# The first attention's probabilities times values: three key blocks of 128, or two of 128 and one of 64-key rests with high and low parts stacked

## The chip, the cores and the metric

The kernel runs on one core of a Trainium2 chip. A core has a matrix engine (TensorE, "PE" in the profile, with its weight loads as "PEld"), a vector engine (VectorE, DVE), a scalar engine (ScalarE, ACT), GpSimd (POOL) and a sync engine (SyncE, SP), which here issues most transfers. The engines run side by side, each through its own queue in order, and wait for one another through semaphores. The metric is the device time of one launch in microseconds; lower is better.

## The reference

One layer of an encoder on 2048 tokens of width 1024: a norm, a projection to queries, keys, values and gates, two attentions, a gated merge, and a feed-forward part. The change lies in the first attention, `windowed_gqa`: 8 query heads of 64 elements share 2 key/value heads, and each query sees the keys at most 128 tokens away.

```python
def block(i):                                   # 128 queries
    qi = qb[:, i]
    ki = lax.dynamic_slice_in_dim(kp, i * A_BLOCK, 3 * A_BLOCK, axis=1)
    vi = lax.dynamic_slice_in_dim(vp, i * A_BLOCK, 3 * A_BLOCK, axis=1)
    dist = jnp.abs(q_pos[:, None] - k_pos[None, :])
    valid = (dist <= A_WINDOW) & (k_pos[None, :] >= 0) & (k_pos[None, :] < s)
    sc = jnp.einsum('bqkgd,bskd->bkgqs', qi, ki) * scale - slopes * dist
    sc = jnp.where(valid, sc, -jnp.inf)
    p = softmax(concatenate([sc, sink_col], -1))[..., :-1]
    return jnp.einsum('bkgqs,bskd->bqkgd', p, vi)
```

A block of 128 queries thus meets 384 keys: the block before it, its own, and the one after it.

## The kernel before, in words

Float32 accuracy is made from pieces: an operand is split into a high part (a copy by ScalarE to a rounded type) and a low part (the rest, a subtraction by VectorE), and the products of the parts are added up in PSUM, the matrix engine's accumulator banks.

The stages follow one another: the input projection for the first half of the tokens (0 to about 360 us), the first attention (to about 646 us), the second attention, and the merge and the feed-forward part. The projection of the second half of the tokens is cut into 68 tiles (24 matmuls of 512 columns each, lines 203 to 205) that serve as filler: `paced` (line 838) hands them out among the attention's blocks, each behind the last product of an earlier block or unit, through the list `done`. In the second attention the first five tiles have no such condition, and the sixth waits for the first unit's last product. The instructions are traced in program order, and an automatic scheduler with a model of times then writes each engine's queue; the order of a queue is thus not the order of the code.

The first attention has 32 units, one for each of two key/value heads `g` and 16 query blocks `i`. `attn_a(g, i)` (line 763) has two phases, and `drive` (line 828) starts the second phase of a unit after the first phase of the unit two later.

- Phase one: the queries are loaded (line 773), reordered by GpSimd (line 774), and put into four groups `u` of 32 queries, each with the four heads of its `g`, so that a group fills 128 rows. Group `u` sees the 288 keys from 32u to 32u + 288 of the 384. Its scores are two matmuls (line 784); VectorE adds the bias and finds the maximum (line 786), ScalarE takes the exponential (line 791), and GpSimd multiplies by the reciprocal of the sum (line 795). The tile `s` has 4 x 384 columns, and what a group doesn't see stays zero.
- Phase two: for each of the three key blocks `c` (two for the first and the last query block), four transposes, one for each `u`, bring 128 keys into the rows and 4 x 128 queries into the columns (line 802). ScalarE copies the high part `ph` (line 805), VectorE makes the low part `pl` (line 806), and two products of 512 columns with the values of that block follow, one for each part (lines 807 and 808). The values' tile holds 64 columns of high and 64 of low parts, so the two halves of the result's rows are added at the end (lines 813 and 814).

Buffers lie in two stacks that grow towards each other in each of SBUF's 128 partitions, one from the left, one from the right. In the first attention the left one holds, above the projection's pages: `ka1`, `va1`, `qraw`, `qa`, `sta`, `sa`, `ya`, `ph`, `pl`, `biasa1`, `byhead`; the right one, next to the filler's weight pools: `biasa0`, `va0`, `ka0`. The second attention's right stack starts at the same weight pools: `masks` (12.5 KB per partition), `kb0` (16), `qb0` (2), `braw0` (2), `biass0` (4), `stb` (0.5), `biass1` (4), `qb1` (2), `qb2` (2), `biasl` (5), `braw1` (2), `kb1` (16). A tile that lies where an earlier one lay waits until that one is no longer read. `biass0` and `biass1` are the short bias tables that GpSimd fills (line 915) for the first and the second unit of the second attention, `qb0` and `qb1` their queries (line 934); its scores are line 947, its scalings line 963, its transposes line 975 and its products line 987.

Of the kernel before, what the change touches and what calls it, by code (L numbers as in the profile page):

```python
# [8 lines left out]
F32 = mybir.dt.float32  # L9
F32R = mybir.dt.float32r  # L10
AF = mybir.ActivationFunctionType
ALU = mybir.AluOpType
# [10 lines left out]
P = 128  # L23
# [72 lines left out]
def encoder_layer(ctx, tc, x, norm_mix, w_in, b_gate, sink, rpb, w_pa, w_pb, w_out,  # L96
                  norm_mlp, w_up, w_down, norm_final, dist_a, mask_b, out):
    nc = tc.nc
    V, A, G, PE, SY = nc.vector, nc.scalar, nc.gpsimd, nc.tensor, nc.sync
# [9 lines left out]
    def pools(stack, side, tags, name):  # L109

        return {t: pool(f"{name}_{t}", side=side, stack=stack) for t in tags}
# [9 lines left out]
    def psum(tag, bufs):  # L121
        n_ps[0] += 1
        return pps[tag].tile([P, 512], F32, tag=tag, bufs=bufs, name=f"{tag}_{n_ps[0]}")
# [3 lines left out]
    def T(pl, shape, dt, tag, bufs):  # L127
        n_t[0] += 1
        pl = pl[tag] if isinstance(pl, dict) else pl
        return pl.tile(shape, dt, tag=tag, bufs=bufs, name=f"{tag}_{n_t[0]}")  # L130


    ident = cp.tile([P, P], F32, name="ident")
# [441 lines left out]
    for p in range(2):  # L575
        t = T(xp, [P, D], F32, "xin", 8).rearrange("p (k c) -> p k c", k=4)
        c = QUADS[2][0]
# [93 lines left out]
    s_h = ExitStack()  # L671
    hpl = [pool(f"hT{n}", side="left", stack=s_h) for n in range(4)]
    s_a = ExitStack()
    ap_ = pools(s_a, "left", ("ka1", "va1", "qraw", "qa", "sta", "sa", "ya", "ph", "pl", "biasa1", "byhead"), "a")
    ap_.update(pools(s_a, "right", ("biasa0", "va0", "ka0"), "a"))
    hp = {}

# [53 lines left out]
    for h in range(4):  # L731
        at = slice(h * A_Q, (h + 1) * A_Q)
# [22 lines left out]
    def load_kv(g, m, behind=None):  # L755
        k, kd = kas[g][:, :, m * (S // 2) : (m + 1) * (S // 2)], ks_a[m][g]
        with tc.issue_after(behind) if behind else nullcontext():
# [2 lines left out]
            SY.dma_start(k[64:128, 1].bitcast(F32), kd[0:64])  # L760
            SY.dma_start(vas[g][:, 8 * m : 8 * m + 8].bitcast(F32), vs_a[m][g])

    def attn_a(g, i):
        c0, c1 = (1 if i == 0 else 0), (2 if i == 15 else 3)
        if bias_a[g] is None:

            with tc.issue_after(shares[2]):
                make_bias_a(g)
        base = (i - 1) * P
        by_head = T(ap_, [P, 4, P], F32, "qraw", 3)  # L770
        q = T(ap_, [P, 4, 4, A_Q], F32R, "qa", 2)
        s = sas[len(began) % 4]
        began.append(SY.dma_start(by_head, qs_a[g][i // 8][:, :, i % 8]).ins)
        G.tensor_copy(out=q.rearrange("p u h q -> p h u q"), in_=by_head.rearrange("p h (u q) -> p h u q", u=4))
        ka, v = kas[g], vas[g]
        st = T(ap_, [P, 8, 4], F32, "sta", 8)
        mx, nm, sm, es, ri = (st[:, k, :] for k in range(5))
        sink_g = sink_p[:, g : g + 1]
        span = [(max(u * A_Q, c0 * P), min(u * A_Q + A_K, c1 * P)) for u in range(4)]
        for u, (lo, hi) in enumerate(span):  # L780
            n = hi - lo
            ps = psum("s", 3)
            for z in range(2):
                PE.matmul(ps[:, :n], q[:, u].rearrange("p h q -> p (h q)"), ka[:, z, base + lo : base + hi],
                          start=z == 0, stop=z == 1)
            V.tensor_tensor_reduce(out=s[:, u, lo:hi], in0=ps[:, :n], in1=bias_a[g][:, lo - u * A_Q : hi - u * A_Q],
                                   scale=1.0, scalar=sink_g, op0=ALU.add, op1=ALU.max, accum_out=mx[:, u : u + 1])
        A.activation(nm, mx, AF.Copy, scale=-1.0)
        A.activation(es, mx, AF.Exp, bias=sink_g, scale=-1.0)
        for u, (lo, hi) in enumerate(span):  # L790
            A.activation(s[:, u, lo:hi], s[:, u, lo:hi], AF.Exp, bias=nm[:, u : u + 1], accum_out=sm[:, u : u + 1])
        V.tensor_tensor(out=sm, in0=sm, in1=es, op=ALU.add)
        V.reciprocal(ri, sm)
        for u, (lo, hi) in enumerate(span):
            share = G.tensor_scalar(s[:, u, lo:hi], s[:, u, lo:hi], ri[:, u : u + 1], 1.0, ALU.mult, ALU.mult)
        shares.append(share.ins)
        yield
        po = psum("av", 1)
        for c in range(c0, c1):
            pt = psum("pt", 2)  # L800
            for u in range(4):
                PE.transpose(pt[:, u * P : (u + 1) * P], s[:, u, c * P : (c + 1) * P], ident)  # L802
            ph = T(ap_, [P, 512], F32R, "ph", 3)
            pl = T(ap_, [P, 512], F32R, "pl", 3)
            A.copy(ph, pt)
            V.tensor_tensor(out=pl, in0=pt, in1=ph.bitcast(F32), op=ALU.subtract)
            PE.matmul(po, v[:, i - 1 + c, :], ph, start=c == c0, stop=False)
            last = PE.matmul(po, v[:, i - 1 + c, :], pl, start=False, stop=c == c1 - 1).ins
        done.append(last)
        t = T(ap_, [64, 512], F32, "ya", 2)  # L810
        t4 = t.rearrange("d (h u q) -> d h u q", h=4, u=4)
        by_u = po.rearrange("p (u h q) -> p h u q", u=4, h=4)
        A.copy(t4, by_u[64:128])
        V.tensor_tensor(out=t4, in0=by_u[0:64], in1=t4, op=ALU.add)
        flush(queue=SY)
        put(y_a[g].rearrange("(h d) t -> d h t", d=64)[:, :, i * P : (i + 1) * P],
            t.rearrange("d (h q) -> d h q", h=4))
# [838 lines left out]
```

## Time and profile before

| | |
|---|---|
| median of 3 runs | 2607.2 us (2606.03 to 2607.28) |
| profiled execution | 2605.6 us, span 2603.8 us |
| granted clock of TensorE | 0.999 |
| busy share of the span | PE 99%, DVE 62%, ACT 47%, POOL 14% |
| first attention, transposes (line 802) | 368 |
| first attention, products (lines 807 and 808) | 92 and 92 |

The span runs from the first to the last instruction of one profiled execution; the device time is a little longer. "Busy" of TensorE counts overlapping matmuls as one stretch, so the distance between the starts of two matmuls tells more than their durations. A group's row gives line, engine, operation, the tiles written and read, the shape and the count, and then either the least, median and greatest duration in ns with the first and last start in us, or the busy time in us with the mean in ns and the idle time before it. A timeline row gives the start, the duration from the first start to the last end of so many like instructions in a row, and, in brackets, the idle time before them and who ended it.

### The profile page before, as it was taken

The page shows a single profiled execution, that of the slowest core. Times are in us where ns is not written, and L with a number is a line of the kernel's source. Part 1 is how long each engine was busy: PE and PEld are TensorE (multiplying, and loading weights), DVE is VectorE, ACT ScalarE, POOL GpSimd, SP SyncE. Part 2 cuts the span into 40 slices and gives each one's busy share as a digit, 9 for nine tenths or more (in the row PEclk, how much of TensorE's full clock was granted, in tenths as well). Part 3 has the DMA queues.
Part 4 walks back from the last instruction along what each step waited for, and adds up shares of the span by engine and source line. Part 5 has one row for each costly group of instructions (what it writes and reads, how often), then busy time and mean ns, then how long its engine had stood idle before and what let it go on. Part 6 is the DMA issues. An engine that isn't in the chain of part 4 may idle for free.

```text
span 2603.8 us, 34627 instructions
## 1 busy us (share of the span) xinstructions
PE 2571.4 (99%) x12140; PEld 2143.3 (82%) x12140; DVE 1608.0 (62%) x2621; ACT 1232.4 (47%) x2261; POOL 368.1 (14%) x493
## 2 busy tenths in 40 slices
PE   8999999999999999999999999999999999999999
PEld 6888788788888888888888888888888888888887
DVE  8865666665544444665478677766656535554766
ACT  5334356666555555542335544644444322323454
POOL 1000124444655541000000000100000000000010
PEclk9999999999999999999999999999999999999999
DMA  5657486465975745865466665854428825445555
GB/s 185 203 155 202 132 260 166 119 167 154 247 212 173 207 140 188 273 202 161 143 198 207 238 222 200 306 173 146 158 100 313 290 97 186 146 148 167 186 193 171
DMA packets 354127, 490.40 MB, mean 188 GB/s; under 512 B 28808, under 2 KB 188808, under 8 KB 351776
## 3 DMA queue, kind: packets, MB, share of 16 engines
q1 hardware_dynamic: 346896, 471.14, 57.6%
q10 hardware_dynamic: 7056, 17.04, 1.8%
q8 instruction: 96, 1.57, 0.2%
q14 instruction: 79, 0.65, 0.1%
HBM read 328.64 MB, written 159.45 MB: 187 GB/s over the span
## 4 chain that ended last, share of the span: by engine, by line
PE 90%; DVE 4%; DMA 2%; ACT 2%; issue 1%; SPq 0%; POOL 0%; DVEq 0%; POOLq 0%; ACTq 0%
PE b L300 15%; PE b L302 15%; PE b L301 15%; PE mm L203 6%; PE mm L205 6%; PE mm L204 6%; PE zb L300 3%; PE zb L302 3%; PE zb L301 3%; PE pt L203 2%; PE pt L204 2%; PE pt L205 2%; PE av L987 2%; PE pt L975 2%; PE s L947 2%; PE pt L802 1%
## 5 line engine op out<-in xcount | busy, mean ns | idle before, releaser
L301 PE MATMUL b<-dwh,dah 128*128 128x512 f32 x896 | 348.5, 389 | 0.0
L302 PE MATMUL b<-dwh,dah 128*128 128x512 f32 x896 | 347.6, 389 | 0.0
L300 PE MATMUL b<-dwh,dah 128*128 128x512 f32 x896 | 339.6, 389 | 0.0
L296 ACT CAST dah<-da 128x1024 fp32r<-128x1024 f32 (+1 forms) x128 | 120.9, 945 | 368.0 <-PE b L302 245.9
L297 DVE TENSOR_TENSOR dah<-da,dah 128x1024 fp32r<-128x1024 f32 (+1 forms) x128 | 139.5, 1090 | 221.3 <-ACT dah L296 216.8
L301 PE MATMUL b<-ubh,uwhlb 128*128 128x512 f32 x592 | 230.3, 389 | 0.0
L300 PE MATMUL b<-ubh,uwhlb 128*128 128x512 f32 x592 | 230.2, 389 | 0.0
L302 PE MATMUL b<-ubh,uwhlb 128*128 128x512 f32 x592 | 229.2, 389 | 0.0
L203 PE MATMUL mm<-hT,whl 128*128 128x512 f32 x544 | 218.6, 402 | 0.0
L205 PE MATMUL mm<-hT,whl 128*128 128x512 f32 x544 | 215.2, 396 | 0.0
L204 PE MATMUL mm<-hT,whl 128*128 128x512 f32 x544 | 214.4, 394 | 0.0
L301 PEld LDWEIGHTS b<-dwh,dah 128*128 128x128 f32 x896 | 168.2, 188 | 35.0
L302 PEld LDWEIGHTS b<-dwh,dah 128*128 128x128 f32 x896 | 168.2, 188 | 34.9
L300 PEld LDWEIGHTS b<-dwh,dah 128*128 128x128 f32 x896 | 168.2, 188 | 34.9
L300 PE MATMUL zb<-zh,zwhl 128*128 128x512 f32 x476 | 186.7, 394 | 8.3 <-DVE zc L293 3.5
L301 PE MATMUL zb<-zh,zwhl 128*128 128x512 f32 x476 | 186.5, 392 | 0.0
L302 PE MATMUL zb<-zh,zwhl 128*128 128x512 f32 x476 | 183.5, 392 | 0.3 <-DVE zwhl L297 0.3
L293 DVE TENSOR_TENSOR uc<-b,uc 128x512 f32<-128x512 f32 x160 | 109.1, 689 | 105.0 <-PE b L302 104.0
L1526 POOL TENSOR_TENSOR st<-st,power 128x1 f32<-128x1 f32 x16 | 13.4, 841 | 925.2 <-DVE st L1525 925.2
L300 PEld LDWEIGHTS b<-ubh,uwhlb 128*128 128x128 f32 x592 | 111.1, 188 | 23.4 <-issue 0.4
L301 PEld LDWEIGHTS b<-ubh,uwhlb 128*128 128x128 f32 x592 | 111.1, 188 | 23.2
L302 PEld LDWEIGHTS b<-ubh,uwhlb 128*128 128x128 f32 x592 | 111.1, 188 | 23.1
(254 smaller groups left out, 5839.3 us busy)
## 6 DMA issues: line engine op xcount, KB each, us to landing
at<-uc SPq DMA_DIRECT2D x224, 256.0 KB
da<-at SPq DMA_DIRECT2D x96, 512.0 KB
dw<-in_w_down_dram SPq DMA_DIRECT2D x160, 256.0 KB
uraw<-in_w_up_dram SPq DMA_DIRECT2D x32, 1024.0 KB
raw<-in_w_in_dram SPq DMA_DIRECT2D x34, 512.0 KB
zraw<-in_w_in_dram SPq DMA_DIRECT2D x16, 1024.0 KB
z<-zg SPq DMA_DIRECT2D x64, 256.0 KB
qraw<-qs_a SPq DMA_DIRECT2D x32, 256.0 KB
```

Source lines behind the costliest of these rows:

```text
L203: PE.matmul(ps, lh, rh, start=first, stop=False)
L204: PE.matmul(ps, lh, rl, start=False, stop=False)
L205: PE.matmul(ps, ll, rh, start=False, stop=last)
L293: return eng.tensor_tensor(out=out, in0=a, in1=b, op=op).ins
L296: A.copy(hi, src)
L297: return eng.tensor_tensor(out=lo, in0=src, in1=hi.bitcast(F32), op=ALU.subtract).ins
L300: PE.matmul(ps, lh, rh, start=first, stop=False, skip_group_check=True)
L301: PE.matmul(ps, lh, rl, start=False, stop=False, skip_group_check=True)
L302: PE.matmul(ps, ll, rh, start=False, stop=last, skip_group_check=True)
L947: PE.matmul(ps[:, :n], q[:, i, :], kv[:, z, B_R0[i] // 4 : (B_R0[i] + B_NR[i]) // 4, 4 * B_C0[j] : 4 * (B_C0[j] + w)], start=z == 0, stop= ...
L975: PE.transpose(pt[:kp, at + (i - i0) * P : at + (i - i0 + 1) * P], s[i][:, rr : rr + kp], ident)
L987: last = PE.matmul(po[:, i0 * P : (i0 + ni) * P], v[:kp, c, :], src[:kp, o : o + ni * P], start=first, stop=(c == 7 and z == 1), skip_grou ...
```

## The change

In phase two, the key blocks 0 to 2 of a query block are regrouped. The middle block is seen by all four groups of queries and stays as it was. Of the first block, the groups 0 and 1 see more than 64 keys and the groups 2 and 3 only keys of its second half; of the last block, the groups 2 and 3 see more than 64 and the groups 0 and 1 only keys of its first half. So a second set of transposes takes the first block for the groups 0 and 1 and the last block for 2 and 3 (`whole`); each block's products then have 256 columns. The third set (`halved`) takes only the 64 keys of the rests: the high parts lie in rows 0 to 63, the low parts in rows 64 to 127 of one tile, and one product of 256 columns multiplies both with `ve`, in which the 64 rows of v stand twice. GpSimd makes `ve` in phase one, with two copies of 64 x 128 elements for each of the two outer blocks. All products are collected in `todo` and stand behind the three sets of transposes in program order. The new pool `ve` (three buffers of 2 x 128 elements per partition, 1 KB each) is the last on the left stack.

```diff
-    ap_ = pools(s_a, "left", ("ka1", "va1", "qraw", "qa", "sta", "sa", "ya", "ph", "pl", "biasa1", "byhead"), "a")
+    ap_ = pools(s_a, "left", ("ka1", "va1", "qraw", "qa", "sta", "sa", "ya", "ph", "pl", "biasa1", "byhead", "ve"), "a")
...
+    def v_rows(g, k, c):
+        return vas[g][64 - 32 * c : 128 - 32 * c, k]
+
...
+        ve = T(ap_, [P, 2, P], F32R, "ve", 3)
+        for c in (0, 2):
+            if c0 <= c < c1:
+                rows = v_rows(g, i - 1 + c, c)
+                for half in (slice(0, 64), slice(64, P)):
+                    G.tensor_copy(out=ve[half, c // 2], in_=rows)
...
-        for c in range(c0, c1):
+        todo = []
+
+        def whole(keys):
             pt = psum("pt", 2)
-            for u in range(4):
+            for u, c in keys:
                 PE.transpose(pt[:, u * P : (u + 1) * P], s[:, u, c * P : (c + 1) * P], ident)
+            at = slice(keys[0][0] * P, (keys[-1][0] + 1) * P)
             ph = T(ap_, [P, 512], F32R, "ph", 3)
             pl = T(ap_, [P, 512], F32R, "pl", 3)
-            A.copy(ph, pt)
-            V.tensor_tensor(out=pl, in0=pt, in1=ph.bitcast(F32), op=ALU.subtract)
-            PE.matmul(po, v[:, i - 1 + c, :], ph, start=c == c0, stop=False)
-            last = PE.matmul(po, v[:, i - 1 + c, :], pl, start=False, stop=c == c1 - 1).ins
+            A.copy(ph[:, at], pt[:, at])
+            V.tensor_tensor(out=pl[:, at], in0=pt[:, at], in1=ph[:, at].bitcast(F32), op=ALU.subtract)
+            for c in sorted({c for _, c in keys}):
+                us = [u for u, cc in keys if cc == c]
+                cs = slice(us[0] * P, (us[-1] + 1) * P)
+                todo.extend((v[:, i - 1 + c, :], t[:, cs], cs) for t in (ph, pl))
+
+        def halved(cs):
+            pt = psum("pt", 2)
+            ph = T(ap_, [P, 512], F32R, "ph", 3)
+            at = slice(0 if 2 in cs else 256, 512 if 0 in cs else 256)
+            for c in cs:
+                for u in (0, 1) if c == 2 else (2, 3):
+                    k = 2 * P if c == 2 else 64
+                    PE.transpose(pt[0:64, u * P : (u + 1) * P], s[:, u, k : k + 64], ident)
+            A.copy(ph[0:64, at], pt[0:64, at])
+            V.tensor_tensor(out=ph[64:P, at], in0=pt[0:64, at], in1=ph[0:64, at].bitcast(F32), op=ALU.subtract)
+            for c in cs:
+                at = slice(0, 256) if c == 2 else slice(256, 512)
+                todo.append((ve[:, c // 2], ph[:, at], at))
+
+        whole([(u, 1) for u in range(4)])
+        whole([(u, 2 * (u // 2)) for u in range(4) if c0 <= 2 * (u // 2) < c1])
+        halved([c for c in (2, 0) if c0 <= c < c1])
+        for n, (rows, p, at) in enumerate(todo):
+            last = PE.matmul(po[:, at], rows, p, start=n == 0, stop=n == len(todo) - 1, skip_group_check=True).ins
```

## The prediction

> **What bounds the kernel now.** I read the page's totals first, then the busy times by stage, then the groups of the first attention.
>
> ```profile
> span 2603.8 us, 34627 instructions
> PE 2571.4 (99%) x12140; PEld 2143.3 (82%) x12140; DVE 1608.0 (62%) x2621; ACT 1232.4 (47%) x2261; POOL 368.1 (14%) x493
> PE 90%; DVE 4%; DMA 2%; ACT 2%; issue 1%; SPq 0%; POOL 0%; DVEq 0%; POOLq 0%; ACTq 0%
> ```
>
> ```profile
> 360.00:646.00 286.00, 280.21 (x1506) 233.50 (x1506) 171.60 (x491) 183.16 (x508) 129.15 (x206) 1.00 0.60 164
> 646.00:668.00 22.00, 21.21 (x124) 18.40 (x123) 11.77 (x32) 12.40 (x30) 11.15 (x10) 1.00 0.95 254
> ```
>
> TensorE is busy 99% of the span and 90% of the chain that ended last is its work; GpSimd is 0% of that chain. The second fence (columns: stretch, length, busy time and count of PE, PEld, DVE, ACT, POOL, granted clock, DMA share, GB/s) shows the first attention at 360 to 646 us and the start of the second. TensorE fills 280.2 of 286 us at a granted clock of 1.00, because projection tiles run between the attention's own matmuls; GpSimd works 129 of the 286. So what TensorE is spared in this stage should come off the whole time, as long as no new stall appears.
>
> ```profile
> L807 PE MATMUL av<-ph,va x92: 387/395/505, 383.3 to 645.7; 128*128 128x512 f32 x92
> ...
> L805 ACT CAST ph<-pt 128x512 fp32r<-128x512 f32 x92 | 53.1, 585 | 51.6 <-PE pt L802 50.8
> L806 DVE TENSOR_TENSOR pl<-pt,ph 128x512 fp32r<-128x512 f32 x92 | 62.8, 688 | 18.4 <-ACT ph L805 17.9
> L813 ACT COPY ya<-av 64x512 f32<-64x512 f32 x32 | 18.7, 583 | 3.7 <-PE av L808 3.1
> L814 DVE TENSOR_TENSOR ya<-av,ya 64x512 f32<-64x512 f32 x32 | 21.8, 680 | 8.6 <-ACT ya L813 8.4
> ```
>
> Each key block of 128 makes one product with the high parts and one with the low parts, so 92 of each: 28 query blocks with three key blocks and 4 edge blocks with two. Durations (395 ns) overlap from one matmul to the next; what counts is how far apart they start.
>
> ```profile
> 432.09 0.39 PE L807 MATMUL av<-ph,va 128*128 128x512 f32 x1
> ...
> 433.02 0.60 PE L802 MATMUL pt<-ident,sa 128*128 128x128 f32 x4
> ...
> 678.25 0.28 PE L987 MATMUL av<-plb,vb 128*128 128x256 f32 x1
> ...
> 678.73 0.49 PE L975 MATMUL pt<-ident,sb 128*128 128x128 f32 x3
> ...
> 639.77 0.44 PE pt L802 x4
> 642.98 0.33 PE pt L975 x3
> ```
>
> Four products of 512 columns lie between 432.09 and 433.02 us: 0.2325 us each. Four of 256 columns, in the second attention, lie between 678.25 and 678.73: 0.12 us each. The last two rows are the chain's pieces of transposes: 0.44/4 and 0.33/3, so 0.11 us each.
>
> **The change, part by part.** (1) *Products.* An inner query block had 6 of 512 columns: 6 x 0.2325 = 1.395 us. It gets 2 of 512 (middle keys), 4 of 256 (outer key blocks, each for the half of the queries that sees it whole) and 2 of 256 (the 64-key rests, where high and low parts share one 128-row product): 2 x 0.2325 + 6 x 0.12 = 1.185 us, 0.21 less. An edge block goes from 4 x 0.2325 = 0.93 to 2 x 0.2325 + 3 x 0.12 = 0.825, 0.105 less. Sum: 28 x 0.21 + 4 x 0.105 = **6.3 us** off TensorE, all on the path.
>
> (2) *Transposes.* 12 per inner block before and after (8 at an edge). Four of them now take 64 columns. The nearest row is the second attention's: at 642.98 three transposes of 96 columns are 0.11 us apart, as are those of 128 at 639.77.
>
> ```profile
> 642.82 0.49 PE L975 MATMUL pt<-ident,sb 128*96 128x128 f32 x3
> ```
>
> So the number of columns loaded doesn't set their spacing, and I take no gain. [...] If some of the spacing did follow the columns, the gain is bounded by half of 0.11 us, 120 x 0.055 = 6.6 us; below, by zero.
>
> (3) *ScalarE and VectorE.* Three copies and three subtractions per inner block before and after. The rest's cover 64 partitions; rows of 64 and 128 partitions take the same (583 against 585, 680 against 688 ns). The subtraction now writes 64 partitions away from what it reads; L813, which reads the upper 64 partitions into the lower, shows no price for that. An edge block has three pairs of fewer columns in place of two: between 0 and one more pair, 1.3 us, four times, off the path. Nothing.
>
> (4) *GpSimd.* Four copies of 64x128 per inner block, two at an edge: 120.
>
> ```profile
> L735 POOL COPY byhead<-sink_t 32x2 f32<-32x2 f32 x4 | 0.7, 179 | 0.1
> L774 POOL CAST qa<-qraw 128x512 fp32r<-128x512 f32 x32 | 19.6, 615 | 53.9 <-issue 40.0 <-PE s L784 5.2 <-DMA qraw<-qs_a 3.2
> ...
> 438.26 1.95 POOL L795 TENSOR_SCALAR sa<-sa,sta 128x288 f32<-128x288 f32 x4 [3.63 <-DVE sta L793]
> 438.32 0.69 DVE L806 TENSOR_TENSOR pl<-pt,ph 128x512 fp32r<-128x512 f32 x1 [0.24 <-ACT ph L805]
> ...
> 454.49 0.60 PE L802 MATMUL pt<-ident,sa 128*128 128x128 f32 x4
> ```
>
> Between 2 elements at 179 ns and 512 at 615, 128 elements come to 179 + 126/510 x 436 = 287 ns: 34 us for all (bounds 120 x 0.179 = 21 and 120 x 0.615 = 74). GpSimd goes from 129 to 163 of 286 us. Behind the copies in its queue stand the softmax scalings (L795). Counting groups, the scalings at 438.26 are the eleventh block's; they end at 440.2, and the transposes that need them start at 454.49. These 14 us cover the 1.15 us of four copies, and also a wait for one of the three buffers, which comes free with the last product three blocks earlier. If that cover were gone, 28 x 1.15 = 32 us is the most it could cost. I take nothing. The copies also wait for v's load, four transfers long landed except at the stage's start, where GpSimd idles for the bias anyway.
>
> (5) *Stalls inside the stage.*
>
> ```profile
> PEld av L808 <- DVE pl L806: 5.1, 13, 0.8
> PE pt L802 <- DVE pl L806: 2.3, 2, 2.0
> PEld pt L802 <- DVE pl L806: 2.3, 1, 2.3
> PE av L808 <- DVE pl L806: 1.4, 5, 0.4
> ```
>
> About 11 us of waits for the low parts. The products now stand behind all three groups of transposes in program order, but as few follow the last low parts (two short ones) as stood ahead of them. The automatic scheduler will order the stage anew; I take the waits as unchanged, with half of 11, 5.5 us, either way.
>
> (6) *Memory.* The new buffers (3 x 1 KB per partition) lie on top of the left stack, where the second attention's right stack reaches down. By the tile sizes its second short bias table lies 37.0 to 41.0 KB from the weight pools, and the second query buffer 41.0 to 43.0.
>
> ```profile
> 580.83 3.08 POOL L915 TENSOR_TENSOR biass<-braw,masks 128x288 f32<-128x288 f32 x3 [3.15 <-DMA braw<-tab]
> 607.05 0.39 DVE L786 CUSTOM_DVE_ANT_0 sa<-s,biasa,byhead 128x160 f32<-128x160 f32 x1 [1.80 <-PE s L784]
> 607.89 0.57 SPq L934 DMA_DIRECT2D qb<-qs_b  x1
> 623.18 0.78 PE L947 MATMUL s<-kb,qb 128*128 128x384 f32 x4
> 630.90 2.14 POOL L963 TENSOR_SCALAR sb<-sb,stb 128x288 f32<-128x288 f32 x4
> 645.91 0.39 PE L808 MATMUL av<-pl,va 128*128 128x512 f32 x1
> 653.87 10.75 DMA kb<-ks_b
> 654.34 0.82 PE L975 MATMUL pt<-ident,sb 128*96 128x128 f32 x6
> 664.66 0.40 PE L947 MATMUL s<-kb,qb 128*128 128x288 f32 x1 [0.79 <-DMA kb<-ks_b]
> ```
>
> The table is filled at 580.83 while the first attention runs; the query load (607.89) comes just behind the last reader of its bias (607.05). So the first attention's top lies in that query buffer now, and 3 KB more covers the bias table too. Both will wait for the last products (645.91): the second unit of the second attention loses its head start. Its path from there: table 3.1 us, scores 1.3, then 9.9 (last scores at 623.18 to scalings done at 633.0), 14.3 in all. Its first transposes (the last three of the six at 654.34, as a unit has 14 and the first unit's 11 others came before) come 8.4 us after the first attention's end, so 5.9 us stick out. Over these stand projection tiles and two other units; the nearest stall that the same release leaves now, head 1's keys, costs TensorE 0.79 us. I take **0.8**, with 0 and 5.9 plus a slow query load as ends.
>
> **Sum.** 2605.6 (the profiled execution, span 2603.8) - 6.3 + 0.8 = 2600.1. That execution is 1.6 us under the median of 2607.2, so the median becomes **2601.7 us**, 0.21% less. About 0.2%, 5.2 us, is what can be told from no change.
>
> **Rivals.**
> - *The head start costs TensorE in full (slower).* DMA is 0.95 busy at 646 to 668 us, and head 1's keys took 10.75 us there. If the second query load lands like that, 10.75 replaces 3.1 and 13.6 us stick out: 2601.7 - 0.8 + 13.6 = 2614.5. It decides for slower once 6.3 + 5.2 = 11.5 us are lost at this place. For: that DMA share, and only a tile or so of filler is free there. Against: the first unit, whose table and queries lie higher, still goes ahead.
> - *The low-part waits grow by half*: 2601.7 + 5.5 = 2607.2, no change. For: the products wait in one queue of eight. *They fall by half*: 2596.2.
> - *GpSimd's copies hold VectorE up.* If each of the 120 delays one subtraction by its 0.287 us and a quarter reaches TensorE: 8.6 us, 2610.3. Against: at 438.32 a subtraction takes 0.69 us, its mean, beside a GpSimd group that began at 438.26. [...]
> - *The half transposes gain too*: at most 6.6 us more, 2595.1. The 96-column row speaks against it.
>
> **How the numbers follow.** Forecast 0.45, its own range 2598 to 2605 (0.30 of it faster, 0.15 within 0.2%); waits fall 0.11; half transposes 0.02; waits grow 0.17; VectorE held up 0.03; lost head start 0.22. Faster 0.43, same 0.35, slower 0.22. The range 2595 to 2614 leaves out about half of the last case and little below.
>
> **What would show it.** Right: products 6 of 256 columns at 0.12 us spacing and 2 of 512; 120 copies near 0.29 us; scalings still well ahead of their transposes; the second bias table filled only after the first attention's last product. Wrong: a copy near 0.6 us with scalings late; TensorE idle over 3 us at 640 to 670 us; half transposes under 0.1 us; projection tiles moved so that TensorE idles later.

## The result, and the profile after

The kernel after takes 2615.47 us (median of 8 runs, 2613.34 to 2618.53), the kernel before, on the same chips, 2608.11 us (8 runs, 2606.03 to 2608.79). The ratio is 1.0029, 95% interval 1.002 to 1.0039: slower by 7.4 us. The forecast was 5.5 us faster, with 2614 as the upper end of its range.

The first view is the page of the kernel after: its span, busy times and the chain that ended last.

```profile
span 2613.2 us, 34929 instructions
PE 2572.9 (98%) x12200; PEld 2147.9 (82%) x12200; DVE 1612.0 (62%) x2625; ACT 1233.0 (47%) x2265; POOL 402.1 (15%) x613
PE 92%; DVE 3%; ACT 1%; DMA 1%; issue 1%; SPq 1%; POOL 0%; DVEq 0%; POOLq 0%; ACTq 0%
```

The profiled execution took 2615.0 us, 9.4 more than that of before. TensorE has hardly more busy time (2572.9 against 2571.4 us) although its products got shorter, so busy time doesn't show what was lost; a 512-column product with high parts, for one, lasted 443 ns on average, where it was 412 before. So I made an account of my own from the trace: for each two consecutive matmuls, the distance of their ends less the spacing that a matmul of that shape has in an undisturbed run of like ones (0.227 us for 512 columns, 0.176 for 384, 0.132 for 288, 0.119 for 256, 0.109 for a transpose). What is left over is TensorE's loss, whatever caused it. Summed by stretch, in us:

```
kernel    0-362  362-650  650-700  700-1060  1060-end
before     18.1     17.2      1.9       7.1       0.6
after      19.7     21.7      9.5      10.1      -1.1
```

The first stretch runs the same order of matmuls in every kernel here and varies from 18.1 to 22.1, so a figure of this account, which is one profiled execution, is good to some two us there. After 362 us it is steadier: before and the two runs below that only add an idle tile to it have 17.2, 17.0 and 17.0 us in the first attention. After 362 us, from before to after: products -6.3, losses of the first attention +4.5, at 650 to 700 us +7.6, at 700 to 1060 us +3.0. The first stretch adds 1.6 and the last takes 1.7. That is +8.7 in all, near the measured 9.4.

Where 650 to 700 us went is seen in the busy times by stretch; the columns are those of the prediction's second fence. First the kernel after, then before.

```profile
640.00:660.00 20.00, 20.00 (x111) 17.44 (x110) 6.76 (x16) 6.93 (x13) 9.65 (x8) 1.00 0.84 219
660.00:680.00 20.00, 15.51 (x76) 13.72 (x75) 9.59 (x30) 10.87 (x30) 5.28 (x8) 0.84 1.04 242
680.00:700.00 20.00, 19.41 (x107) 16.28 (x106) 8.71 (x23) 11.30 (x31) 18.18 (x21) 0.98 1.01 237
```

```profile
660.00:680.00 20.00, 19.21 (x120) 17.07 (x119) 11.51 (x33) 13.73 (x36) 11.03 (x15) 1.00 1.07 252
```

At 660 to 680 us TensorE makes 76 matmuls in place of 120, and its granted clock there is 0.84 in place of 1.00. The timeline of after, on several engines, tells how this comes about.

```profile
621.16 0.58 SPq L968 DMA_DIRECT2D qb<-qs_b  x1
...
646.65 1.99 SPq L968 DMA_DIRECT2D qb<-qs_b  x2
...
650.08 0.28 PE L842 MATMUL av<-ph,ve 128*128 128x256 f32 x1
650.45 3.06 POOL L949 TENSOR_TENSOR biass<-braw,masks 128x288 f32<-128x288 f32 x3 [10.08 <-PE av L842]
...
659.55 4.93 SPq L968 DMA_DIRECT2D qb<-qs_b  x1
...
669.04 0.97 PE L981 MATMUL s<-kb,qb 128*128 128x512 f32 x4
674.50 0.82 PE L981 MATMUL s<-kb,qb 128*128 128x288 f32 x2 [4.49 <-issue]
675.12 0.41 PE L1021 MATMUL av<-phb,vb 96*128 96x256 f32 x1
...
682.50 0.28 PE L1021 MATMUL av<-phb,vb 96*128 96x256 f32 x1
```

Before, three query loads of the second attention were issued between 600 and 625 us (the last at 624.23), and the second short bias table was filled at 580.83. Now one is issued in that time, the next two at 646.65, and the table is filled at 650.45, right behind the first attention's last product, after GpSimd has stood 10.08 us for it. TensorE then idles 4.49 us before 674.50, and works until about 681 with 0.41 us per 256-column matmul where 0.28 is usual.

The row names no releaser for this idle stretch ("issue"), but the times of the transfers in the trace do tell. The scores at 674.50 are those of the fifth unit. Three query buffers take turns, so its query goes into the second unit's buffer and can be loaded only behind the second unit's scores. These now end at 659.28 us; the load is issued at 659.55 and is complete at 674.41, 0.06 us before the fifth unit's first weight load. Head 1's keys, which that unit needs too, had been complete at 671.69. Before, the second unit's scores ended at 623.73, and the same load was issued at 624.23 and complete at 628.35.

In the first attention itself, the groups of after (first fence) and its waits (second fence: engine and line that waited, who ended it, us in total, times, the longest):

```profile
L783 POOL CAST ve<-va 64x128 fp32r<-64x128 f32 x120 | 35.0, 292 | 19.3 <-PE av L842 14.0
...
L831 PE MATMUL pt<-ident,sa 128*64 128x128 f32 x120 | 18.3, 272 | 2.6 <-DVE pl L818 2.4
L842 PE MATMUL av<-ph,ve 128*128 128x256 f32 x59 | 13.5, 306 | 3.9 <-DVE ph L833 3.9
L842 PEld LDWEIGHTS av<-ph,ve 128*128 128x128 f32 x60 | 9.6, 188 | 6.2 <-DVE ph L833 6.0
```

```profile
PEld av L842 <- DVE ph L833: 6.0, 9, 1.1
PE av L842 <- DVE ph L833: 3.9, 9, 0.8
```

The waits for low parts now stand at the stacked products (`ve`), which can't begin before the subtraction that writes the low half of their operand. Before, the two rows that answer to these came to 5.1 and 1.4 us.

### The profile page after: what moved, and what is told of

Same layout as the page of the kernel before. It is cut to its first block, busy times and chain, and to the rows that moved or that the text cites. A ratio compares the mean times of both kernels' runs of the same rounds, so it can differ in the third digit from the quotient of the medians.

```text
span 2613.2 us, 34929 instructions
## 1 busy us (share of the span) xinstructions
PE 2572.9 (98%) x12200; PEld 2147.9 (82%) x12200; DVE 1612.0 (62%) x2625; ACT 1233.0 (47%) x2265; POOL 402.1 (15%) x613
## 4 chain that ended last, share of the span: by engine, by line
PE 92%; DVE 3%; ACT 1%; DMA 1%; issue 1%; SPq 1%; POOL 0%; DVEq 0%; POOLq 0%; ACTq 0%
PE b L300 16%; PE b L302 15%; PE b L301 15%; PE mm L203 6%; PE mm L205 6%; PE mm L204 6%; PE zb L300 3%; PE zb L302 3%; PE zb L301 3%; PE pt L203 2%; PE pt L204 2%; PE pt L205 2%; PE av L1021 2%; PE pt L1009 2%; PE s L981 2%; PE av L842 1%
```

## The experiments

Three groups: the memory, the order and content of the products, and what in a block makes it wait.

**The memory by itself.** The kernel before gets a tile of 3 KB on top of the left stack that holds nothing and lives until the last block's result.

```diff
-    ap_ = pools(s_a, "left", (..., "biasa1", "byhead"), "a")
+    ap_ = pools(s_a, "left", (..., "biasa1", "byhead", "pad"), "a")
...
+    pad = T(ap_, [P, 3 * 256], F32, "pad", 1)
+    G.memset(pad[:, 0:1], 0.0)
...
+        if g == 1 and i == 15:
+            V.tensor_copy(out=pad[0:64, 0:1], in_=t[:, 0:1])
```

> The kernel before, with an idle tile of 3 KB per partition on top of the first attention's left stack (one element set at the start, one written after the last block's result), so that only the memory of the change is there. Theory M (the lost head start of the second attention's second unit is what cost the change its gain): its second bias table is filled only after about 646 us, TensorE loses 7 to 10 us between 650 and 760 us, and the time is 6 to 10 us above before. Rival O (the new order of transposes and products inside the first attention costs it): no more than 1 us above before. Rival G (GpSimd's copies): likewise no change.

Measured: 2617.12 us, ratio to before 1.0037 (1.0025 to 1.005), where before had 2608.41 on these chips: 8.7 us for memory alone, without one changed instruction of the attention. The losses are 17.0 in the first attention, as before, 9.3 at 650 to 700 and 10.3 at 700 to 1060 us, as after. Both late stretches of the account are thus to be had from memory alone.

The same with 1 KB, which covers the second query buffer but not the bias table:

```diff
-    pad = T(ap_, [P, 3 * 256], F32, "pad", 1)
+    pad = T(ap_, [P, 256], F32, "pad", 1)
```

> The kernel before with an idle tile of 1 KB instead of 3 KB on top of the left stack: it reaches into the second unit's query buffer, not into the bias table. Theory M with the query alone as a full cause: the table is filled near 580 us, the query is loaded only after about 646 us, and the time is 6 to 10 us above before, as with 3 KB. Rival (the bias table is what cost): no more than 2 us above before.

Measured: 2617.73 us, 1.0036 (1.0024 to 1.0048). The query buffer is enough; the table, which the prediction put first, isn't needed for the loss. The timeline of this kernel:

```profile
621.44 0.58 SPq L938 DMA_DIRECT2D qb<-qs_b  x1
...
650.87 0.57 SPq L938 DMA_DIRECT2D qb<-qs_b  x1
652.40 0.57 SPq L938 DMA_DIRECT2D qb<-qs_b  x1
```

One load is issued near 621 us here, as in after; the others wait until the first attention has ended. TensorE's idle stretch (3.59 us, and 3.98 with 3 KB) ended with GpSimd's scalings here, not with a query load as in after; what held these up wasn't followed.

**The kernel after with its top as low as before's.** First with two buffers in place of three for `pl` and `ve`, so that the stack is as high as before:

```diff
-        ve = T(ap_, [P, 2, P], F32R, "ve", 3)
+        ve = T(ap_, [P, 2, P], F32R, "ve", 2)
...
-            pl = T(ap_, [P, 512], F32R, "pl", 3)
+            pl = T(ap_, [P, 512], F32R, "pl", 2)
```

> The changed kernel with two buffers instead of three for the low parts and for the doubled rows of v, which brings the top of the left stack back to where it was before. Theory M: the second bias table is filled near 580 us again, the losses after 650 us are gone, and the time is 7 to 10 us under the changed kernel's, so 0 to 5 us under before. Rival O: the losses between 350 and 650 us stay and the time stays within 2 us of the changed kernel's, some 7 us above before. Rival G: likewise.

Measured: 2613.28 us, 1.002 (1.0011 to 1.0029), 2.2 us under after, where Theory M had 7 to 10. The losses at 650 to 700 us stayed, 9.1. The timeline says why:

```profile
583.61 3.04 POOL L949 TENSOR_TENSOR biass<-braw,masks 128x288 f32<-128x288 f32 x3
...
621.52 0.58 SPq L968 DMA_DIRECT2D qb<-qs_b  x1
...
650.76 0.56 SPq L968 DMA_DIRECT2D qb<-qs_b  x1
652.09 0.55 SPq L968 DMA_DIRECT2D qb<-qs_b  x1
```

The table is filled early again, but the query buffer still lies under `ve`, the topmost tile, which is read until the last product. Before, the topmost tiles were `byhead` and the bias, done with earlier. TensorE idled 5.47 us here, to 675.85, and the fifth unit's query was complete at 675.75. So height alone isn't it: what counts is which tile lies on top. Then `ve` below `ph`, with the two buffers kept:

```diff
-    ap_ = pools(s_a, "left", (..., "ya", "ph", "pl", "biasa1", "byhead", "ve"), "a")
+    ap_ = pools(s_a, "left", (..., "ya", "ve", "ph", "pl", "biasa1", "byhead"), "a")
```

> The kernel with fitted buffers (two for the low parts, two for the doubled rows), the doubled rows moved below the high parts in the left stack, so that the tiles on top of it are the bias and the head constants at their old places. Theory M, now with both covered tiles (bias table and query buffer of the second unit): that query is loaded near 610 us again, the losses after 650 us go back from 19 to 9 us, and the time is 8 to 10 us under the changed kernel's, 0 to 3 us under before. Rival: something else in the change delays the second attention, and the time stays where the fitted kernel's was, 4 to 7 us above before.

Measured: 2609.57 us, 1.0005 (0.9996 to 1.0013), 5.9 us under after, less than the 8 to 10 expected. The timeline and then the busy times by stretch:

```profile
609.09 0.57 SPq L968 DMA_DIRECT2D qb<-qs_b  x1
620.78 0.57 SPq L968 DMA_DIRECT2D qb<-qs_b  x1
625.41 0.56 SPq L968 DMA_DIRECT2D qb<-qs_b  x1
```

```profile
660.00:680.00 20.00, 18.84 (x113) 16.54 (x112) 11.35 (x33) 15.40 (x40) 9.87 (x12) 1.00 1.07 254
```

Three loads are early again, TensorE makes 113 matmuls at a clock of 1.00, and the loss at 650 to 700 us is 3.7. The 10.1 at 700 to 1060 us and the 21.5 in the first attention remained, so memory doesn't explain these here.

**The order of the products.** The kernel after with each group's products right behind its own transposes:

```diff
         whole([(u, 1) for u in range(4)])
+        products()
         whole([(u, 2 * (u // 2)) for u in range(4) if c0 <= 2 * (u // 2) < c1])
+        products()
         halved([c for c in (2, 0) if c0 <= c < c1])
+        products()
```

> The changed kernel with each group's products right behind its transposes in program order, the memory as in the change. Theory M: the same head start is lost, and the time is within 2 us of the changed kernel's, some 7 us above before. Rival O: the waits between 350 and 650 us go back by about 4.5 us, and with them the time.

Measured: 2617.62 us, 1.0038 (1.0025 to 1.005); losses of the first attention 26.8. That is worse than behind all transposes (21.7), the opposite of Rival O. And the reverse, the kernel before with its six products behind all its transposes:

```diff
-            PE.matmul(po, v[:, i - 1 + c, :], ph, start=c == c0, stop=False)
-            last = PE.matmul(po, v[:, i - 1 + c, :], pl, start=False, stop=c == c1 - 1).ins
+            todo.extend(((c, ph), (c, pl)))
+        for n, (c, p) in enumerate(todo):
+            last = PE.matmul(po, v[:, i - 1 + c, :], p, start=n == 0, stop=n == len(todo) - 1).ins
```

> The kernel before with its six products of a block behind all of the block's transposes in program order, nothing else. Theory M: within 2 us of before. Rival O: 4 us or more above before, with the waits for low parts between 350 and 650 us at 21 us rather than 17.

Measured: 2607.16 us, 0.9997 (0.9989 to 1.0006); losses 16.3 against 17.2. The queue of products at the end of a block costs nothing in that kernel.

**GpSimd's copies.** The kernel after with the doubled rows made once for all blocks, 4 copies in place of 120:

```diff
-        ve = T(ap_, [P, 2, P], F32R, "ve", 3)
-        for c in (0, 2):
...
+        if not ves:
+            ves.append(T(ap_, [P, 6, P], F32R, "ve", 1))
+            for c in (0, 2):
+                rows = v_rows(1, 1, c)
```

> The changed kernel with the doubled rows of v made once for all blocks instead of for each, in a buffer of the same 3 KB that lives as long; 116 of GpSimd's 120 copies and their waits are left out, and the rests of all blocks are multiplied with the rows of one block. Rival G (the copies in GpSimd's queue cost the extra waits inside the first attention): the losses between 362 and 650 us fall from 21.7 to about 17 us and the time by 4 us or more. Theory M with the rest from the shape of the products: both stay within 2 us of the changed kernel's, some 7 us above before.

Measured: 2614.28 us, 1.0024 (1.0015 to 1.0033); losses of the first attention 22.2 against 21.7. This kernel leaves out 116 copies and multiplies the rests of all blocks with the rows of one. The copies are not what the products wait for.

**Another order of the groups.** From the kernel with `ve` below `ph`: the stacked rests second, the outer blocks last, their high parts' products ahead of the low parts':

```diff
-            for c in sorted({c for _, c in keys}):
...
+            for t in (ph, pl):
+                for c in sorted({c for _, c in keys}):
...
         whole([(u, 1) for u in range(4)])
-        whole([(u, 2 * (u // 2)) for u in range(4) if c0 <= 2 * (u // 2) < c1])
         halved([c for c in (2, 0) if c0 <= c < c1])
+        whole([(u, 2 * (u // 2)) for u in range(4) if c0 <= 2 * (u // 2) < c1])
```

> As f_low, with the stacked rests second instead of last, and the outer blocks' products with the high parts ahead of those with the low parts. If the waits inside the first attention are for the last group's low parts, which a stacked product needs from its first column on: two of the last group's products can start a subtraction (0.69 us) earlier, the losses between 362 and 650 us fall by 2 to 5 us under f_low's and the time by as much. If they are not: within 1.5 us of f_low.

Measured: 2612.48 us, 1.0015 (1.0006 to 1.0023); losses of the first attention 25.6, 4.1 more than with the rests last; after 650 us 2.3 and 7.4, as in before. That lies outside both expectations: putting the stacked group elsewhere didn't help its stage but made it worse.

**Are the spared products worth their time, or were they a cover?** From the same kernel, the outer blocks' high-part products made twice:

```diff
-                todo.extend((v[:, i - 1 + c, :], t[:, cs], cs) for t in (ph, pl))
+                twice = (ph, ph, pl) if len(us) == 2 else (ph, pl)
+                todo.extend((v[:, i - 1 + c, :], t[:, cs], cs) for t in twice)
```

> The kernel with the small buffers and ve below ph, but each outer block's high-part product of 256 columns is made twice (outer keys' high parts count double in the output, which is therefore not the reference's): 60 more products of 0.12 us, 7.2 us more work on TensorE, which puts the products' time back to 0.9 us above that of before. Theory C (the products were themselves the cover under which the last group's copy and subtraction ran, so that what they got shorter came back as waits): TensorE's losses at 362 to 650 us fall from 21.5 to about 17, as in before (17.2), and the median rises by only 2 to 3 us, 2609.6 to about 2612. Rival S (the waits come with the stacked last group, which needs copy and subtraction before any of its products, however much stands ahead of it): losses stay at 21 to 22 us and the time rises by the whole 7.2, to about 2617.

Measured: 2616.39 us, 1.0034 (1.0022 to 1.0047), 6.8 us above the kernel without them; losses 21.7 against 21.5. The cover theory falls: sixty products of 256 columns cost what 60 x 0.12 = 7.2 us says, and the waits stay. By the same price the change's products did spare some 6 us.

The rest group's copy and subtraction in two halves, so that the first stacked product could begin sooner:

```diff
-            A.copy(ph[0:64, at], pt[0:64, at])
-            V.tensor_tensor(out=ph[64:P, at], in0=pt[0:64, at], in1=ph[0:64, at].bitcast(F32), op=ALU.subtract)
             for c in cs:
                 at = slice(0, 256) if c == 2 else slice(256, 512)
+                A.copy(ph[0:64, at], pt[0:64, at])
+                V.tensor_tensor(out=ph[64:P, at], in0=pt[0:64, at], in1=ph[0:64, at].bitcast(F32), op=ALU.subtract)
```

> The kernel with the small buffers and ve below ph, with the rest group's one copy and one subtraction of 512 columns made as two of 256 each, one pair for each outer block, so that the first stacked product's parts are ready some 0.5 us sooner. Theory C (the last group's chain of transposes, copy, subtraction, product is what the products wait for): losses at 362 to 650 us fall from 21.5 to 17 to 19.5, time 2609.6 to 2605.5 to 2608. Rival S2 (ScalarE and VectorE's queues, not that chain's length, set the waits): losses 21 to 24 us, since two more instructions each add fixed time to both engines, time 2609 to 2613.

Measured: 2626.16 us, 1.0069 (1.0056 to 1.0082), losses 37.6: outside both expectations. The waits of this kernel:

```profile
ACT ph L833 <- DVE ph L834: 17.4, 17, 2.1
DVE ph L834 <- ACT ph L833: 13.5, 21, 2.9
PEld av L841 <- DVE ph L834: 8.1, 10, 2.1
```

ScalarE's second copy waited for VectorE's first subtraction; both write the one tile `ph`, though other parts of it. So the halves ran one behind the other and the chain got longer, not shorter. (The edge blocks of after show what a half takes: 382 ns for ScalarE's copy and 419 for VectorE's subtraction with 256 columns, against 578 and 684 with 512.) The run doesn't test what it was made for, but shows that a longer chain there cost TensorE at once (37.6 against 21.5 us of losses).

**Edge blocks.** From the kernel with `ve` below `ph`, the four edge blocks in two groups as before:

```diff
+        edge = c1 - c0 == 2
+        if not edge:
+            ve = T(ap_, [P, 2, P], F32R, "ve", 2)
...
         whole([(u, 1) for u in range(4)])
+        if edge:
+            whole([(u, 2 if i == 0 else 0) for u in range(4)])
+        else:
+            whole([(u, 2 * (u // 2)) for u in range(4)])
+            halved([2, 0])
```

> The kernel with the small buffers and ve below ph, with the four edge blocks made as before: two groups of 128 keys with products of 512 columns, no rest, no copies of v's rows; inner blocks stay in three groups. TensorE's work rises by 4 x 0.105 = 0.4 us. Theory E (the waits grew where edge blocks got a third group and, at the stage's start, nothing else covers it; 2.4 us of the growth lie at 380 to 400 us): losses at 380 to 400 fall from 5.2 to about 2.8, those at 362 to 650 from 21.5 to about 19, time 2609.6 to about 2607.5. Rival (the inner blocks' groups do it): losses stay at 21 to 22, time 2609.5 to 2610.5.

Measured: 2604.43 us (11 runs), 0.9983 (0.9974 to 0.9992) of before's 2608.36 (15 runs): 3.9 us faster than before, the best of all kernels here, and 5.1 us better than with three groups at the edges (the two ratios' intervals, 0.9996 to 1.0013 and 0.9974 to 0.9992, don't meet). That is more than Theory E expected, but not where it put it: the first attention's losses fell only from 21.5 to 20.9 (from 5.3 to 4.7 at 362 to 400 us). The larger part lies later, 3.7 to 2.2 at 650 to 700 and 10.1 to 7.0 at 700 to 1060 us.

**The stacking.** The kernel after with the low parts of the rests in a tile of their own and two products of 64 rows each:

```diff
-            V.tensor_tensor(out=ph[64:P, at], in0=pt[0:64, at], in1=ph[0:64, at].bitcast(F32), op=ALU.subtract)
-            for c in cs:
-                at = slice(0, 256) if c == 2 else slice(256, 512)
-                todo.append((ve[:, c // 2], ph[:, at], at))
+            pl = T(ap_, [P, 512], F32R, "pl", 3)
+            V.tensor_tensor(out=pl[0:64, at], in0=pt[0:64, at], in1=ph[0:64, at].bitcast(F32), op=ALU.subtract)
+            for p in (ph, pl):
+                for c in cs:
+                    at = slice(0, 256) if c == 2 else slice(256, 512)
+                    todo.append((ve[0:64, c // 2], p[0:64, at], at))
```

> The kernel after, with the rests unstacked: their low parts go to a tile of their own and high and low parts make two products of 64 rows each, the high ones first, so the first two need only ScalarE's copy, as in before; the copies into the upper half of ve stay but are not read. TensorE's work is 60 products of 0.12 us, 7.2 us, above that of after, the same as in the run with the outer high parts twice. Theory S (the stacked products, which need copy and subtraction, made the waits grow): losses at 362 to 650 fall from 21.7 to 17 to 18.5, time 2615.5 + 7.2 - 4 = about 2618.5. Rival E (not the stacking): losses 21 to 22.5, time about 2622.5.

Measured: 2635.52 us, 1.0105 (1.0089 to 1.012), losses 36.3: 13 us beyond the higher of the two expectations. The timeline shows a price that nobody had put in:

```profile
439.66 0.28 PE L844 MATMUL av<-ph,va 128*128 128x256 f32 x1
439.77 0.28 PE L844 MATMUL av<-pl,va 128*128 128x256 f32 x1
...
440.49 0.51 PE L793 MATMUL s<-ka,qa 128*128 128x288 f32 x2
440.93 0.50 PE L844 MATMUL av<-ph,ve 64*128 64x256 f32 x2
441.36 0.80 PE L793 MATMUL s<-ka,qa 128*128 128x288 f32 x4
```

Two scores of 288 columns are 0.132 us apart, so the next matmul should start 0.26 us behind 440.49; the 64-row product starts 0.44 behind it. Two products of 256 columns should be followed after 0.24 us; the scores come 0.43 us later. Over the first attention there were 55 changes from 128 to 64 rows and 55 back. The median distance of ends was 0.312 us on the way in, where 0.119 is the spacing, and on the way back 0.259 before a transpose (spacing 0.109) and 0.330 before a score (0.132). At these prices the changes make some 19.8 of the 36.3 us, and 16.5 are left, near before's 17.2. The run leaned towards Theory S, but couldn't decide it.

So the stacking was taken away once more, with all matmuls at 128 rows: from the kernel with edge blocks as before, the rest group takes whole key blocks, and `ve` falls away.

```diff
-    ap_ = pools(s_a, "left", (..., "ya", "ve", "ph", "pl", "biasa1", "byhead"), "a")
+    ap_ = pools(s_a, "left", (..., "ya", "ph", "pl", "biasa1", "byhead"), "a")
...
-            halved([2, 0])
+            whole([(u, 2 - 2 * (u // 2)) for u in range(4)], high_first=True)
```

> The kernel with edge blocks as before, and in the inner blocks the rest group unstacked, with all 128 rows kept: whole key blocks are transposed for it and high and low parts make two products of 256 columns each, the high ones first; ve and its copies fall away, and the memory is that of before. TensorE's work is 56 products of 0.12 us, 6.7 us, above that of the run with edge blocks as before; no matmul of 64 rows is in it. Theory S (the stacked products, which need copy and subtraction, made the waits of the inner blocks grow): losses at 362 to 650 us fall from 20.9 to 16 to 18, time 2604.4 + 6.7 - 4 = about 2607. Rival T (three groups with all products behind them, or the blocks' new order in the queue, did it): losses 20 to 22, time about 2611.

Measured: 2611.52 us, 1.0014 (1.0005 to 1.0023). The losses of the first attention are 18.2, against 20.9 with the stacked rests: 2.7 us of the growth go with the stacking, a little less than Theory S had. The added products, the missing copies and the third buffer of `pl`, which differ too, had each moved these losses by 0.5 us at most in the runs above (21.7 for 21.5, 22.2 for 21.7, 21.6 for 21.7). The time, though, is Rival T's (about 2611), 4.5 us above what Theory S gave; the account finds 2.9 us of it after 1060 us (1.8 against -1.1), where the change has no part. So it is the account that speaks for the stacking, not the time. The waits of this kernel and, in the second fence, of the one with stacked rests:

```profile
PEld av L830 <- DVE pl L813: 3.1, 10, 0.5
...
PEld av L830 <- ACT ph L812: 1.1, 3, 0.7
```

```profile
PEld av L846 <- DVE ph L834: 4.4, 7, 1.1
PEld av L846 <- DVE ya L852: 1.7, 6, 0.4
...
PEld av L846 <- DVE pl L819: 1.4, 5, 0.3
PEld av L846 <- ACT ph L818: 1.1, 3, 0.6
```

The wait for the stacked operand (4.4 us, up to 1.1 at a time) is gone, and shorter ones for plain low parts (3.1, up to 0.5) stand in its place.

The account of all kernels, from which the figures above are taken:

```
kernel                                362-650  650-700  700-1060
before                                   17.2      1.9       7.1
before, 3 KB on top                      17.0      9.3      10.3
before, 1 KB on top                      17.0      8.0      10.3
before, products behind transposes       16.3      1.8       7.1
after                                    21.7      9.5      10.1
after, small buffers                     21.6      9.1      10.1
after, small buffers, ve below ph        21.5      3.7      10.1
  ... rests second                       25.6      2.3       7.4
  ... outer high parts twice             21.7      2.1      10.1
  ... copy and subtraction in halves     37.6      5.2      10.3
  ... edge blocks as before              20.9      2.2       7.0
      ... and rests not stacked          18.2      2.0       7.0
after, products behind each group        26.8      9.2      10.1
after, doubled rows made once            22.2      7.4      10.1
after, rests as 64-row products          36.3      6.6       9.2
```

## Why the prediction was wrong

It had the sign wrong, and the time lies 1.5 us above its range. Step by step:

- **(6) Memory is the step that failed.** It saw the mechanism, the first attention's top over the second unit's bias table and queries, and found 5.9 us that stick out; then it took 0.8, from the stall that the same release left before (head 1's keys, 0.79 us). In place of the 0.8 stand 7.6 us at 650 to 700 us. Memory alone measured 8.7 us when added to before, and taking it off the kernel after gave 5.9 back. Three things were wrong. The step followed the second unit alone, to its first transposes; TensorE stood still at the fifth unit's scores, whose query has to wait for the second unit's buffer. The filler tiles were taken as cover, but TensorE idled 4.49 us, and the half speed granted from 673.77 to 680.60 us, around the end of this idle time, cost about 3 more. And the bias table was taken as what comes late; one KB over the query buffer alone did the same. What the trace had to be read for was the last reader of each tile at the top: `byhead` and the bias are done with nearly 40 us before the end, `ve` only with the last product. Of the signs named for being wrong, idle time over 3 us came, but from 670.01 us on and not at 640 to 670.
- **(5) The waits in the stage** were taken as unchanged, with 5.5 us either way; they grew by 4.5. The reason given there, that as few matmuls follow the last low parts as stood ahead of them, missed that the stacked products need ScalarE's copy and VectorE's subtraction before any of them can begin. Taking the stacking away brought 2.7 us back. The sum of 11 us also counted some waits twice, once for the weight load and once for its matmul: both rows of 2.3 us tell of a wait that ended at 488.7 us. About 1 us remains for the groups' new shape (18.2 against 17.2) and 0.6 for the edge blocks, both near what the account can tell.
- **(3) Edge blocks** were held to be free, with up to one pair of copy and subtraction four times "off the path". Undoing them gave 5.1 us. Only 0.6 of it lies in the first attention; what they change in the later order of the work was not found.
- **(1) Products**: right. Their spacing is 0.119 and 0.232 us in the trace of after, and 60 added ones cost 6.8 us where 7.2 follow from the spacing. The gain was on the path, and other losses took it away.
- **(2) Half transposes**: right. They are 0.109 us apart, as are those of 128 columns, and no gain is seen.
- **(4) GpSimd's copies**: right in size (292 ns for the estimated 287, 35.0 us for 34) and in effect, by the run with 4 of them (22.2 against 21.7 us of losses), which also speaks against the rival in which they hold VectorE up; the subtractions' mean stayed 688 ns (684 for the rests).
- **The rivals.** "The head start costs TensorE in full" named 2614.5 us and was nearest, but its sum isn't what happened: it had 13.6 us at this place, and 7.6 were lost there at 650 to 700 us. With the waits' 4.5 and the 3.0 after 700 us the time came out close to it by another road. Its condition, 11.5 us lost at this place, was thus not met. "Waits grow by half" had its 5.5 us nearly right, though not by its reason, the products in one queue: a queue of six cost nothing in the kernel before. Neither case held the two together, which is how the range came to be too low.

What stays open: the losses at 700 to 1060 us take one of two values, 7.0 to 7.4 or 9.2 to 10.3. Memory over the query buffer brings the higher one, but freeing it doesn't bring the lower one back, while the edge blocks or the groups' order do. The automatic scheduler orders each kernel's second attention anew; which of its choices makes the 3 us wasn't followed.

## What to carry to other kernels

A buffer added at the end of a stack can have a price in the next stage (8.7 us here for 3 KB that held nothing): before adding it, ask which of the next stage's tiles lies there, what is loaded into it early, and when the topmost tile is last read; here the doubled rows cost 5.9 us less when they lay deeper and `ve` and `pl` made do with two buffers each. When high and low parts are stacked into one operand, the product waits for both (6.0 us in all for the weight loads of the stacked rests in after), so count what covers the longer chain. And a change that pays in the inner case need not be made at the edges: with `ve` deeper, leaving them alone was worth 5.1 us, and took the kernel from 1.7 us slower than before to 3.9 us faster. That is a thing to try rather than a rule, since only 0.6 us of it lies in the stage itself and the cause of the rest is open.

## What the runs showed of the hardware

Two things that I had not expected.

In after, a pause of TensorE cost more than its length. 4.49 us of idle time end at 674.50; from then to about 681 us a matmul of 256 columns took 0.41 us, 0.21 apart, and the usual 0.28, 0.12 apart, only from 682.50. The granted clock of 660 to 680 us is 0.84, where before has 1.00. The clock's own record in the trace has half speed from 673.77 to 680.60, 6.8 us. So about 3 us went on top of the 4.49, and the two make up the 7.6 of this stretch. In the kernel with 1 KB on top, 3.59 us of idle time were followed by 3.4 us at half speed (674.51 to 677.92), and the granted clock of 660 to 680 us is 0.91. The length of a pause alone didn't tell whether half speed follows: 2.91 us of idle time up to 267.31 in after were followed by it (granted clock 0.50 from 267.59 to 271.00 us), and the 2.91 us up to 266.99 in before were not (1.00 to 275 us). Why the clock fell in the one case and not in the other wasn't shown.

Changing the number of rows of a matmul between 128 and 64 cost 0.15 to 0.2 us each way in the kernel with the rests as 64-row products (0.312 for 0.119 us, 0.259 for 0.109, 0.330 for 0.132), some 19.8 us for its 110 changes. Transposes of 64 columns at 128 rows paid nothing of the kind in after (0.109 us apart). So stacking two 64-row operands into one of 128 rows, as the change does, spared more than one product here: it spared the changes.
